# Mask codes of 16 rows instead of 40 in a tree attention kernel

## The chip, the cores and the metric

The kernel runs on one core of a Trainium2 chip. The time is that of the device for one execution, in microseconds (us). Before the change it is 133.4 us, the median of three runs (132.78 to 133.66).

The core's engines work side by side and are kept in step by semaphores: TensorE for matmuls and transposes (PE in the profile, its weight loads PEld), VectorE (DVE), ScalarE (ACT), GpSimd (POOL) and SyncE (SP). Transfers to and from the main memory run on 16 DMA engines; here nearly all of them are issued by POOL.

## The reference: attention along a tree

There are 8 batches of 12 heads, so 96 heads, each with 512 positions of 64 values. The positions are the nodes of a binary tree, numbered as in a heap: the parent of node n is (n - 1) // 2. A query may look at itself and at its ancestors only:

```python
    for i in range(seq):
        mask[i, i] = 1
        parent = i
        while parent > 0:
            parent = (parent - 1) // 2
            mask[i, parent] = 1

    scores = np.einsum('bhqd,bhkd->bhqk', Q, K) * scale
    scores = scores + (1 - mask) * (-1e9)
    weights = np.exp(scores - np.max(scores, axis=-1, keepdims=True))
    weights = weights / (np.sum(weights, axis=-1, keepdims=True) + 1e-10)
    return np.einsum('bhqk,bhkd->bhqd', weights, V)
```

So of 512 x 512 scores per head at most ten in each row count.

## The kernel before

**Heads and pairs.** The work goes in 48 pairs of heads (`i` in the code). The two heads of a pair, `a` = 0 and 1, lie beside each other in the partitions: head 0 has its 64 dimensions in partitions 0 to 63, head 1 in 64 to 127. Four pairs share loads of eight heads.

**Which scores are computed.** The 512 nodes are split by the remainder modulo 4 into four slots of 128. For every query two tiles of 128 keys are enough. The first, in `scores1`, is the top of the tree, nodes 0 to 127. The second, in `scores2`, is a tile of four blocks of 32 nodes in which all the deeper ancestors of the queries of a slot lie; which four blocks it takes depends on the slot (`UNITS`, `TILE2`). Of the four blocks, two neighbours hold nodes from 128 to 255 and the other two hold nodes from 256 up, so that a query finds at most one of its nodes in either two.

**The mask as a matmul.** The mask is not added by VectorE. Before the keys are multiplied with the queries, a product of two small code matrices is put into the same accumulator: `k1code` with `q1code` (L484) under the first scores (L489), `k2code` with `q2code` (L509) under the second (L515). A code product is zero where the key is an ancestor of the query or the query itself, and a large negative number elsewhere (multiples of 2048), so that the exponential gives zero. In the first scores a key's code is its path from the root, as signs, in seven rows, and the negative length of that path in an eighth. In the second scores the code of before has ten rows for each of the four slots, nine signs of the path and one length: 40 rows. The codes are one constant, `tree_codes`, of `CODE_ROWS` rows and 1280 columns. It is loaded once (L183), copied by ScalarE to partitions 64 and up for the second head (L209), and POOL makes a reordered copy `qcoarse` of the query codes for heads 32 and up (L237).

**The stages of a pair.**
- Transpose, T (`transpose`): K and Q come in with nodes in the partitions; TensorE turns them against a permuted unit matrix (L345, L367, L388) into the buffer `kqp`, and VectorE copies that into `kq` (L426, L434, L440).
- Scores, S: per pair two code products of 512 columns (L484), two key products of 512 (L489), two code products of 480 (L509) and eight key products of 160 or 64 columns (L515), always in the order head 0, head 1. ScalarE takes the exponential of the first scores (L500) and of the second (L531).
- Values, V: 12 products of 65 columns with all 128 queries of a slot and 8 with halves of 64 queries (L542); the 65th column sums the weights. VectorE takes the reciprocal (L575) and multiplies (L580).

**What sets the order.** The order on each engine is written by hand. The main loop goes over the turns `i`; a string of letters gives the steps of a turn: by `STV` the scores of pair i are followed by the transposes of a pair ahead and the values of pair i - 1 (`SVT` in the first turns, `FIRST` in the very first). The score buffers `s1` and `s2`, the transposes' `kqp` and the values' `ob` exist once each, so a stage waits for the engine that empties the buffer. Further work of VectorE is to spread V into the order of the tiles (L298, shared with ScalarE and POOL) and, once in four pairs, to lay the two heads' keys beside each other (`Kbeside`, L322). POOL has a list of its own: loads (L249, L259), its share of the V copies, the same laying beside of Q (`Qbeside`, L322), and the stores of the output (L589), which stay 64 heads behind the loads. Its transfers go through eight lanes, and a new one waits for a lane.

Of the kernel before, what the change touches and what calls it, by code (L numbers as in the profile page):

```python
# [9 lines left out]

CODE = 2048.0
CODE_ROWS = 40
NOUT = 10
BEHIND = 64
LANES = 8
# [11 lines left out]
TOP = 6  # L27
TILE2 = (0, 12, 10, 2)

SELF = (2, 3, 2, 3)  # L30
ORDER = (2, 0, 3, 1)
PLACE = (1, 3, 0, 2)
# [28 lines left out]
def _nodes(u0):  # L61
    return np.concatenate(
        [4 * (ROWS[kind] + np.arange(32)) + t for kind, t in UNITS[u0:u0 + 4]]
    )


def _path(n):

    return [1.0 if c == "1" else -1.0 for c in bin(n + 1)[3:]]


def _mask_codes():

    k1 = np.zeros((64, 128), np.float32)
    q1 = np.zeros((64, 4, 128), np.float32)
    k2 = np.zeros((64, 128), np.float32)  # L80
    q2 = np.zeros((64, 4, 128), np.float32)

    def key(codes, row, bits, col, node):
        path = _path(node)
        assert len(path) <= bits
        codes[row:row + len(path), col] = np.array(path) * CODE
        codes[row + bits, col] = -len(path) * CODE

    def query(codes, row, bits, col, node):
        path = _path(node)[:bits]  # L90
        codes[(slice(row, row + len(path)),) + col] = path
        codes[(row + bits,) + col] = 1.0

    for c, node in enumerate(_nodes(TOP)):
        key(k1, 0, 7, c, node)
    for t in range(4):
        for c, node in enumerate(_nodes(TILE2[t])):
            key(k2, 10 * t, 9, c, node)
        for p in range(128):
            node = 4 * p + t  # L100
            query(q1, 0, 7, (PLACE[t], p), node)
            if p >= 32:
                query(q2, 10 * (SELF[t] if p < 64 else t), 9, (PLACE[t], p), node)
    return np.concatenate([k1, q1.reshape(64, -1), k2, q2.reshape(64, -1)], axis=1)


# [8 lines left out]
def kernel(  # L115
# [31 lines left out]
    perm_dram = nc.inline_tensor(_eye_twice().astype(ml_dtypes.bfloat16), name="tree_eye")  # L147
    code_dram = nc.inline_tensor(
        _mask_codes()[0:CODE_ROWS].astype(ml_dtypes.bfloat16), name="tree_codes"
    )  # L150

# [23 lines left out]
    def first_load(eng, name, src):  # L175
        eng.dma_start(
            out=first[name][:, :, :, :].rearrange("p h t d -> p h (t d)"), in_=src[:, 0:2, :]
        )
# [3 lines left out]
    first_load(nc.scalar, "Q", Qr)  # L182
    nc.sync.dma_start(out=codes[0:CODE_ROWS, :], in_=code_dram.ap())  # L183
    eye = ptile[:, 0:256]
# [23 lines left out]

    nc.scalar.copy(out=codes[64:64 + CODE_ROWS, :], in_=codes[0:CODE_ROWS, :])  # L209

# [23 lines left out]
    def code_order(rows):  # L234
        for n, code in enumerate((q1code, q2code)):
            src = code[rows:rows + CODE_ROWS, :].rearrange("r (t p x) -> r x t p", t=4, x=4)
            nc.gpsimd.tensor_copy(out=qcoarse[rows:rows + CODE_ROWS, n, :, :, :], in_=src)  # L237

# [230 lines left out]
    def query_codes(i, a, n, lo, hi):  # L469

        g = i // GP
        rows = slice(64 * a, 64 * a + CODE_ROWS)
        if g in COARSE:
# [347 lines left out]
```

## Time and profile before

| | |
|---|---|
| median of three runs | 133.4 us (132.78 to 133.66) |
| the profiled execution | 134.61 us |
| its span, first to last instruction | 132.7 us |
| TensorE busy | 116.3 us in 2131 matmuls, mean clock 0.984 |
| VectorE, ScalarE, POOL busy | 106.0, 98.4 and 93.2 us |
| read from and written to main memory | 37.92 and 12.58 MB |
| first and last scores begin | 7.13 and 122.49 us |
| last instruction of VectorE ends | 126.8 us |

The profile is one execution, taken by the hardware. Times in it are microseconds from the first instruction. In a group, the form such as `40*128 40x512` gives first the rows and columns of the weights, then the partitions and columns of the stream. "x64 | 12.5, 386 | 0.0" are 64 instructions, 12.5 us busy in sum, 386 ns for one, and no idle time before them. The ends of matmuls are modelled, so consecutive matmuls overlap in it; the distance from one start to the next says how long one really holds the engine. The view of the chain follows the work that ended last backwards; there a step takes the time from the end of the step before.

### The profile page before, as it was taken

Reading aid. Unit: us, or ns where it says so; the run is one execution under the profiler, and the core shown is the slowest. Engines: PE = TensorE matmul, PEld = TensorE weight load, DVE = VectorE, ACT = ScalarE, POOL = GpSimd, SP = SyncE. Lnnn points to the kernel's source line nnn. Section 1 sums busy time; section 2 is a strip of 40 time slices with the busy share of each in tenths; the row PEclk is TensorE's granted clock in tenths of the full one; section 3 lists DMA queues with packets and bytes.
Section 4 is the critical chain, followed back from the end, with each engine's and each line's share of the span. In section 5 each row is a group of like instructions: output and inputs, shape, how many; then the busy total and the mean of one; then the engine's idle time right before and its main releaser. Section 6 shows DMA issues by size and latency. Waiting matters only on the chain.

```text
span 132.7 us, 4957 instructions
## 1 busy us (share of the span) xinstructions
PE 116.3 (88%) x2131; PEld 82.0 (62%) x2131; DVE 106.0 (80%) x216; ACT 98.4 (74%) x153; POOL 93.2 (70%) x140
## 2 busy tenths in 40 slices
PE   6989998898978989999996999999999989999700
PEld 2343765575746667776674786877776757757500
DVE  2427778789896988999999999999999999983610
ACT  4359499799897778799697587887877776889600
POOL 6977735446499999999697974249999998626200
PEclk9999999999999999999999999999999999999985
DMA  3999999999999999999999999999999999999991
GB/s 107 219 183 194 199 194 198 195 198 197 204 203 211 202 203 199 209 206 205 211 200 213 201 342 233 202 332 245 204 316 263 269 396 388 391 381 404 388 357 41
DMA packets 29431, 32.20 MB, mean 243 GB/s; under 512 B 1210, under 2 KB 22330, under 8 KB 29410
## 3 DMA queue, kind: packets, MB, share of 16 engines
q0 software_dynamic: 28112, 30.68, 114.6%
q1 hardware_dynamic: 738, 0.76, 1.6%
q10 hardware_dynamic: 560, 0.46, 1.1%
q8 instruction: 16, 0.26, 0.7%
q14 instruction: 5, 0.04, 0.1%
HBM read 37.92 MB, written 12.58 MB: 380 GB/s over the span
## 4 chain that ended last, share of the span: by engine, by line
DMA 43%; POOL 20%; PE 14%; DVE 9%; ACT 6%; issue 5%; ACTq 0%; POOLq 0%
DMA qst<-in_Q_dram 21%; DMA kst<-in_K_dram 11%; DMA vst<-in_V_dram 11%; POOL vt L298 7%; PE ob L542 5%; DVE of L580 3%; ACT e L531 2%; ACT e L500 2%; DVE vt L298 2%; POOL out_dram L589 2%; POOL qcoarse L237 2%; POOL vst L249 2%; POOL Qbeside L322 2%; PE s L484 2%; PE s L489 1%
## 5 line engine op out<-in xcount | busy, mean ns | idle before, releaser
L500 ACT ACTIVATE e<-s 128x1024 bf16<-128x1024 f32 x48 | 49.2, 1025 | 22.6 <-PE s L489 22.2
L531 ACT ACTIVATE e<-s 128x384 bf16<-128x384 f32 (+1 forms) x80 | 40.8, 556 | 0.0
L542 PE MATMUL ob<-vt,e 128*128 128x65 bf16 (+1 forms) x940 | 37.0, 197 | 2.1 <-DVE of L580 1.3
L542 PEld LDWEIGHTS <-e 128*128 128x128 bf16 (+1 forms) x960 | 30.9, 102 | 8.2 <-DVE of L580 3.4
L580 DVE TENSOR_TENSOR of<-ob,rec 128x512 f32<-128x512 f32 x44 | 30.4, 692 | 1.5
L298 POOL COPY vt<-vst 32x256 uint32<-32x256 uint32 (+1 forms) x52 | 26.2, 503 | 5.5 <-DMA vst<-in_V_dram 3.1
L298 DVE COPY vt<-vst 32x512 uint32<-32x512 uint32 (+4 forms) x52 | 24.7, 475 | 2.8 <-DMA vst<-in_V_dram 1.4
L515 PEld LDWEIGHTS <-kq 64*128 64x128 bf16 x384 | 16.1, 106 | 7.0
L589 POOL DMA_DIRECT2D out_dram<-of x22 | 16.7, 764 | 4.6 <-DVE of L580 2.9
L489 PE MATMUL s<-kq 64*128 64x512 bf16 x96 | 18.6, 379 | 1.0 <-DVE kq L440 0.5
L515 PE MATMUL s<-kq 64*128 64x64 bf16 (+1 forms) x384 | 17.9, 210 | 0.0
L322 POOL COPY Qbeside<-qst 128x1024 uint32<-128x1024 uint32 x9 | 9.7, 1074 | 7.1 <-DMA qst<-in_Q_dram 6.8
L440 DVE COPY kq<-kqp 128x1024 bf16<-128x1024 bf16 x16 | 11.0, 685 | 4.6 <-PE kqp L345 4.4
L575 DVE RECIPROCAL rec<-ob 128x8 f32<-128x8 f32 x47 | 9.4, 199 | 6.0 <-PE ob L542 5.4
L249 POOL DMA_DIRECT2D vst<-in_V_dram x14 | 12.4, 884 | 1.7 <-DVE rec L575 0.7
L484 PE MATMUL s<-qcoarse,codes 40*128 40x512 bf16 x64 | 12.5, 386 | 0.0
L509 PE MATMUL s<-qcoarse,codes 40*128 40x480 bf16 x64 | 12.0, 364 | 0.4 <-ACT e L531 0.2
L509 PEld LDWEIGHTS <-codes 40*128 40x128 bf16 x96 | 7.1, 95 | 8.1 <-issue 2.8
L426 DVE COPY kq<-kqp 128x1024 bf16<-128x1024 bf16 x16 | 11.1, 692 | 1.2 <-PE kqp L388 0.6
L298 ACT COPY vt<-vst 64x512 uint32<-64x512 uint32 (+4 forms) x22 | 11.2, 508 | 0.8 <-DMA vst<-in_V_dram 0.4
L434 DVE COPY kq<-kqp 128x1024 bf16<-128x1024 bf16 x16 | 10.9, 682 | 0.4 <-PE kqp L367 0.3
L367 PE MATMUL kqp<-mixed,Kbeside 128*128 128x128 bf16 x128 | 9.9, 220 | 1.1 <-DVE Kbeside L322 0.8
(43 smaller groups left out, 124.6 us busy)
## 6 DMA issues: line engine op xcount, KB each, us to landing
out_dram<-of POOLq DMA_DIRECT2D x22, 512.0 KB, 9.7
vst<-in_V_dram POOLq DMA_DIRECT2D x11, 512.0 KB, 12.4
qst<-in_Q_dram POOLq DMA_DIRECT2D x10, 512.0 KB, 13.7
kst<-in_K_dram POOLq DMA_DIRECT2D x9, 512.0 KB, 13.5
kst<-in_K_dram POOLq DMA_DIRECT2D x4, 256.0 KB, 9.2
qst<-in_Q_dram POOLq DMA_DIRECT2D x2, 256.0 KB, 9.0
out_dram<-ol POOLq DMA_DIRECT2D x2, 256.0 KB, 7.2
kst<-in_K_dram POOLq DMA_DIRECT2D x3, 128.0 KB, 7.8
```

Source lines behind the costliest of these rows:

```text
L249: return nc.gpsimd.dma_start(out=kept[b][:, h0 % size:h0 % size + n, :, :].rearrange("p h t d -> p h (t d)"), in_=src[:, h0:h0 + n, :],)
L298: return copy(out=dst, in_=src)
L322: copy(out=dst, in_=src)
L484: nc.tensor.matmul(out=columns(g, sp[:, a, :], 0, 512), lhsT=k1code[64 * a:64 * a + CODE_ROWS, :], rhs=query_codes(i, a, 0, 0, 512), start ...
L489: nc.tensor.matmul(out=columns(g, sp[:, a, :], 0, 512), lhsT=keys(i, a, TOP), rhs=queries(i, a, 0, 512), start=False, stop=True,)
L500: nc.scalar.activation(out=dst, in_=src, func=AF.Exp, scale=scale)
L509: nc.tensor.matmul(out=columns(g, flat[:, a, :], 32, 512), lhsT=k2code[64 * a:64 * a + CODE_ROWS, :], rhs=query_codes(i, a, 1, 32, 512), s ...
L515: nc.tensor.matmul(out=columns(g, flat[:, a, :], lo, hi), lhsT=keys(i, a, TILE2[t]), rhs=queries(i, a, lo, hi), start=False, stop=t == 1,)
L531: nc.scalar.activation(out=dst, in_=src, func=AF.Exp, scale=scale)
L542: nc.tensor.matmul(out=ob[lo:hi, a, 65 * t:65 * t + 65], lhsT=e[:, a, PLACE[t], lo:hi], rhs=vt[:, head(i, a) % VB, tile_v, 0:D + 1], **flags,)
L580: nc.vector.tensor_tensor(out=dst, in0=o4[:, a:a + n, :, 0:D], in1=rec[:, a:a + n, :, :].to_broadcast([P, n, 4, D]), op=ALU.mult,)
L589: return eng.dma_start(out=Or[:, h:h + n, :], in_=ofs[h // KB][:, h % KB:h % KB + n, :, :].rearrange("p h t d -> p h (t d)"),)
```

## The change

The number of code rows goes from 40 to 16. The first scores keep their code of eight rows. In the second scores a key's code is no longer its path: it is the place of its column within a block of 32, as five signs, and a weight for its block. Blocks 0 and 1 share rows 0 to 4 for the signs, blocks 2 and 3 share rows 5 to 9, and rows 10 to 13 hold one weight for each block; 14 rows are in use. The query's code has, for a block in which it has an ancestor, the signs of that ancestor's place and a weight of -5, and for any other block a weight of -7. The sum is zero for the ancestor and at most -2 x 2048 for any other key. All of it is computed on the host when the kernel is built; the code matrices have other numbers, and the instructions that read them work on 16 partitions in place of 40. Lines below the function move down by 12.

```diff
-CODE_ROWS = 40
+CODE_ROWS = 16
@@ _mask_codes
-    def key(codes, row, bits, col, node):
+    for c, node in enumerate(_nodes(TOP)):
         path = _path(node)
-        assert len(path) <= bits
-        codes[row:row + len(path), col] = np.array(path) * CODE
-        codes[row + bits, col] = -len(path) * CODE
-
-    def query(codes, row, bits, col, node):
-        path = _path(node)[:bits]
-        codes[(slice(row, row + len(path)),) + col] = path
-        codes[(row + bits,) + col] = 1.0
-
-    for c, node in enumerate(_nodes(TOP)):
-        key(k1, 0, 7, c, node)
+        assert len(path) <= 7
+        k1[:len(path), c] = np.array(path) * CODE
+        k1[7, c] = -len(path) * CODE
+
+    def bits(place):
+        return np.array([1.0 if place >> n & 1 else -1.0 for n in range(5)])
+
+    for c in range(128):
+        block, place = divmod(c, 32)
+        row = 5 * (block // 2)
+        k2[row:row + 5, c] = bits(place) * CODE
+        k2[10 + block, c] = CODE
     for t in range(4):
-        for c, node in enumerate(_nodes(TILE2[t])):
-            key(k2, 10 * t, 9, c, node)
         for p in range(128):
             node = 4 * p + t
-            query(q1, 0, 7, (PLACE[t], p), node)
-            if p >= 32:
-                query(q2, 10 * (SELF[t] if p < 64 else t), 9, (PLACE[t], p), node)
+            path = _path(node)[:7]
+            q1[:len(path), PLACE[t], p] = path
+            q1[7, PLACE[t], p] = 1.0
+            if p < 32:
+                continue
+            up = [node]
+            while up[-1] > 0:
+                up.append((up[-1] - 1) // 2)
+            q2[10:14, PLACE[t], p] = -7.0
+            tile_nodes = _nodes(TILE2[SELF[t] if p < 64 else t])
+            found = [divmod(c, 32) for c in range(128) if tile_nodes[c] in up]
+            assert len({block // 2 for block, _ in found}) == len(found)
+            for block, place in found:
+                row = 5 * (block // 2)
+                q2[row:row + 5, PLACE[t], p] = bits(place)
+                q2[10 + block, PLACE[t], p] = -5.0
```

## The prediction

> **What bounds the kernel now.** I read the page first (busy shares, the row of DMA engines, the chain), then the busy time by stretches, and then the chain of waits at the end and the timeline of VectorE. The page shows no idle engine:
>
> ```profile
> span 132.7 us, 4957 instructions
> ...
> PE 116.3 (88%) x2131; PEld 82.0 (62%) x2131; DVE 106.0 (80%) x216; ACT 98.4 (74%) x153; POOL 93.2 (70%) x140
> ...
> DMA  3999999999999999999999999999999999999991
> ...
> DMA 43%; POOL 20%; PE 14%; DVE 9%; ACT 6%; issue 5%; ACTq 0%; POOLq 0%
> ```
>
> The DMA engines carry packets in every slice, and the chain passes through transfers most often. But such a share says little of who waits, so I go by stretches. Columns: stretch, its length, then busy time with instruction counts of PE, PEld, DVE, ACT, POOL, the granted clock, the DMA share and GB/s:
>
> ```profile
> 21.00:36.00 15.00, 13.81 (x312) 9.95 (x312) 12.57 (x27) 13.30 (x20) 6.86 (x10) 1.00 1.45 198
> 36.00:49.00 13.00, 10.96 (x200) 7.93 (x194) 11.15 (x22) 10.89 (x15) 12.47 (x21) 1.00 1.26 204
> 49.00:73.50 24.50, 22.86 (x422) 16.73 (x420) 22.92 (x42) 19.48 (x32) 22.08 (x34) 1.00 1.23 206
> 73.50:116.70 43.20, 41.87 (x806) 31.72 (x801) 41.30 (x81) 33.69 (x57) 33.39 (x50) 1.00 1.14 292
> ```
>
> From 49 to 116.7 us VectorE is busy 64.2 of 67.7 us and TensorE 64.7 (its ends are modelled, so that is a little too much). VectorE's beat can be read from the copy that it makes once in four pairs:
>
> ```profile
> 80.09 0.83 DVE L322 COPY Kbeside<-kst 128x1024 uint32<-128x1024 uint32 x1
> ...
> 107.71 1.00 DVE L322 COPY Kbeside<-kst 128x1024 uint32<-128x1024 uint32 x1
> ```
>
> With two more between them (four in all), three periods take 27.62 us, so 9.2 us for four pairs. TensorE's own beat, with nothing to wait for, stands in the chain (start, duration, step; a step's time runs from the end of the step before):
>
> ```profile
> 109.60 0.79 PE ob L542 x20
> ...
> 112.50 0.32 PE s L484 x2
> 112.83 0.22 PE s L489 x2
> 113.04 0.21 PE s L509 x2
> 113.25 0.21 PE s L515 x8
> 113.46 0.55 PE kqp L388 x8
> 114.01 0.61 PE ob L542 x20
> ```
>
> One pair is the sum of the last six rows, 2.12 us, and four pairs are 8.48. So in the long middle VectorE is the bound by a small margin (9.2 against 8.48, that is 0.18 us a pair); before it the loads and POOL's copies are, where POOL is busy 12.47 of 13 us from 36 to 49; and from 109.60 us on the chain lies on TensorE, later on ScalarE too.
>
> **The change, part by part.** No instruction is added, removed or moved: the order on every engine is the same. What changes is the height of the code operands, 40 rows to 16, in the code transfer, its copies and the code products.
>
> ```profile
> L484 PE MATMUL s<-qcoarse,codes 40*128 40x512 bf16 x64 | 12.5, 386 | 0.0
> ...
> L237 POOL COPY qcoarse<-codes 40x512 bf16<-40x512 bf16 x4 | 2.8, 736 | 0.0
> ```
>
> *The code transfer and its copies.* The first code product against ScalarE's copy:
>
> ```profile
> 4.64 1.26 ACT L209 COPY codes<-codes 40x1280 bf16<-40x1280 bf16 x1 [1.42 <-DMA codes<-tree_codes]
> ...
> 6.78 0.41 PE L345 MATMUL kqp<-ptile,kst 128*64 128x128 bf16 x8 [0.25 <-DVE kq L440]
> ...
> 7.13 0.39 PE L484 MATMUL s<-codes 40*128 40x512 bf16 x2
> ```
>
> The transfer of 40 rows becomes one of 16 and may land earlier than at 4.64; ScalarE's copy waits 1.42 us for it and ends at 5.90. That gains nothing: the first code product starts at 7.13, 1.2 us later, behind transposes that waited for VectorE.
>
> The copies have the same elements per partition, only fewer partitions. For ScalarE two rows show that the partitions don't count:
>
> ```profile
> L298 ACT COPY vt<-vst 64x512 uint32<-64x512 uint32 x7 | 4.4, 627 | 0.1
> ...
> L298 ACT COPY vt<-vst 32x512 uint32<-32x512 uint32 x5 | 3.1, 627 | 0.1
> ```
>
> For POOL's four copies no such pair stands in the trace. Bounds: nothing, or in proportion to the rows, 24/40 of 2.8 = 1.7 us gained in a stretch where POOL issues loads into DMA engines that are full anyway. I take 0, by the ScalarE rows, the nearest; from the ends I keep −1.7.
>
> *The code products.* The streams stay 512 and 480 columns, so the matmuls themselves stay as long, and two of them run side by side already (the row at 7.13 has two in 0.39 us, where one is 0.386). What does change is the part of the array that they occupy. The built program places every product in a tile by its rows and columns. Until now codes (40 rows) and keys (64 rows) both took the 64 by 128 tile, one at row 0, one at row 64. With 16 rows the codes take a 32 by 128 tile, so the four groups of a pair's scores now go 32, 64, 32, 64 rows where they went 64, 64, 64, 64.
>
> What does such a change of tile cost? The trace has three a pair, and the chain above prices them. L484 and L489 stream the same 512 columns, yet the first takes 0.32 and the second 0.22: L484 follows value products in a 128 by 64 tile, L489 follows its own kind. So 0.10 us. L388 streams 8 x 128 = 1024 columns; at L489's 512 in 0.22 that is 0.44, and it takes 0.55: 0.11 for 64 by 128 to 128 by 128. L542 has 12 products of 65 columns and 8 that go in pairs, 1040 columns or 0.45 us, and takes 0.61: 0.16 for one change inside it, its small starts included. L509, which follows its own kind of tile, takes 0.21 for 480 columns, which is 0.206 by the same rate: no price. So 0.10 to 0.16 for each change, and I take 0.10, since two of three lie there and the new ones sit between long streams as at L484. No row has a change between 64 and 32 rows; its bounds are 0 and 0.16.
>
> The Trainium skill ("TensorEngine Tiling (Array Packing)", Tiling Modes) says that a change of tiling mode, not of the tile alone, drains TensorE, and lists 64 and 32 rows as different modes; the three prices above agree with the drain, and no run here shows the 64 to 32 case yet. It speaks against this change, and by it the sum stays the one below.
>
> New changes per pair: before L489, before L509, before L515. L484 had one and keeps one. That is 3 x 0.10 = 0.30 us a pair, and 48 x 0.30 = 14.4 us of TensorE time in all. Nothing is removed from it.
>
> **How much of it reaches the end.** By stretches, with these starts of a pair's scores (pairs 0 as quoted, 15, 44):
>
> ```profile
> 49.03 0.39 PE L484 MATMUL s<-codes 40*128 40x512 bf16 x2
> ...
> 116.67 0.39 PE L484 MATMUL s<-qcoarse,codes 40*128 40x512 bf16 x2
> ```
>
> *Middle, pair 15 to 44*: 29 pairs in 67.64 us. TensorE's beat becomes 2.12 + 0.30 = 2.42, four pairs 9.68, above VectorE's 9.2: the bound changes hands. 29 x 2.42 = 70.2 us, so +2.5 if TensorE never waits. It will still wait: in the turn with the extra copy VectorE gets some 0.8 us of work more, and the next value products need the buffer that it empties. From that I take 0.2 us per four pairs, 7 times, 1.4 us: now the wait there is about 9.2 − 8.48 = 0.7, and TensorE's beat grows by 0.3 on each of two turns around it. That makes +3.9. Bounds: +2.5, and 29 x 0.30 = +8.7 where every wait of today stays.
>
> *Beginning, pair 0 to 15*: 41.9 us, 15 x 0.30 = 4.5 added. TensorE's waits are for loads, and the chain there runs through them:
>
> ```profile
> 11.48 9.48 DMA qst<-in_Q_dram
> ...
> 27.58 0.24 PE s L489 x2
> ...
> 32.73 0.38 PE s L509 x2
> 33.10 0.20 PE s L515 x8
> ...
> 34.79 0.24 PE s L489 x2
> ...
> 49.89 13.96 DMA vst<-in_V_dram
> ```
>
> Between the two transfers the chain passes four of the new changes (L489, L509, L515, L489), 0.4 us; the rest lies in waits for transfers that don't start earlier or later by it. Because loads are issued behind buffers that TensorE empties, a little more leaks through: I take +0.9, bounds 0 and 4.5.
>
> *End, from pair 44*: no transposes are left, and the chain alternates between ScalarE and TensorE:
>
> ```profile
> 117.09 0.42 PE s L489 x2
> ...
> 118.51 0.88 ACT e L531 x2
> ...
> 119.43 0.38 PE s L509 x2
> 119.81 0.20 PE s L515 x8
> ...
> 121.06 0.24 PE s L489 x2
> ...
> 123.22 0.38 PE s L509 x2
> 123.60 0.21 PE s L515 x8
> ```
>
> L489, L509 and L515 stand in it twice each: 6 x 0.10 = +0.6. The last values, norms and stores only shift.
>
> Sum: 0.9 + 3.9 + 0.6 = +5.4 us. The profiled execution took 134.6 us (span 132.7 and 1.9 around it), which lies 1.2 above the median of 133.4; against itself it would be 140.0, against the median 138.8.
>
> **The rivals.**
>
> *A, the other side: no drain between 64 and 32 rows.* If a 32-row tile is only half of the 64-row one to the array, a pair stays at 2.12 us. More generally, VectorE's 9.2 us for four pairs hide the change as long as 8.48 + 12c stays below it, so up to c = 0.06 us; below that only six changes in the end count, at most 0.4 us, and POOL's shorter copies may take 1.7 us off. For it: no row shows such a change. Against it: three different changes of tile, in rows and in columns, all cost 0.10 or more. Time 133.4, range 131.7 to 133.8; not slower.
>
> *B, the drain costs what I think, but the waits swallow it.* The chain touches TensorE little before 109.60 us (14% of the whole span). If VectorE and the transfers go on setting the beat up to there, only what the chain passes counts: four new changes early, three in each of the three pairs from 109.60 on, six at the end, 19 x 0.10 = +1.9, so 135.3. For it: the chain's shares and the DMA row. Against it: from 73.5 us TensorE is idle for only 1.3 us of 43.2, and 9.68 is more than 9.2; there is hardly a wait to hide in.
>
> *C, nothing is hidden.* All waits are fixed distances behind TensorE's own work (a single score buffer, a single value buffer, loads behind buffers), and the 14.4 us add in full: 147.8. For it: the buffers are single. Against it: VectorE's 0.7 us in four pairs is a bound of its own and is overtaken, not added to; C is the forecast with that step failed.
>
> **How the numbers follow.** The forecast, 138.8, reaches from 136.5 (0 + 2.5 + 0.6) to 143.6 (0.9 + 8.7 + 0.6) by its own bounds and has 0.68. A has 0.10, B 0.13, and C with all that lies above 143.6 has 0.09; a price of 0.16 in place of 0.10 is in these, since it would lead there. The range of 134.8 to 145.0 leaves out A (0.10), an edge of B, and most of C, about 0.2 in all. About 1% is what a measurement of this kernel can tell from no change. Slower by over 1% (above 134.7): forecast, C and nearly all of B, 0.88. Within 1%: most of A and an edge of B, 0.10. Faster by over 1%: A with POOL's 1.7 us reaching the end, 0.02.
>
> **What the new profile would show.** L489, L509 and L515 as steps of the chain at about 0.32, 0.31 and 0.31 us where TensorE runs without a wait, L484 still at 0.32, and a pair at 2.42; the duration of L484 in its group unchanged (386 ns), since the drain lies between instructions. VectorE with small waits for TensorE in the middle, where it has none now, and the four-pair beat of its extra copy at 9.7 to 9.9. POOL's L237 still at 0.7 us each. I would be wrong if L489 stays at 0.22 behind L484 (A), if the beat stays at 9.2 (B), or if it reaches 10.4 (C).

## The result and the profile after

The changed kernel takes 139.29 us (median of six runs, 138.32 to 141.41) against 133.31 (132.78 to 134.67): by the medians it is slower by 6.0 us, where 5.4 was forecast (138.8 us in all). The ratio is 1.040, with a 95% interval of 1.036 to 1.045, which is 5.4 us (4.8 to 6.0). Here and below a ratio compares only the faster executions of both kernels (within 1.5% of the fastest of their kind), so it is not the quotient of the medians. The profiled execution took 139.53 us.

The page of the changed kernel, its heads and the rows of slices (tenths busy; the last is GB/s):

```profile
span 137.7 us, 4957 instructions
...
PE 129.5 (94%) x2131; PEld 81.0 (59%) x2131; DVE 106.7 (77%) x216; ACT 98.4 (71%) x153; POOL 92.5 (67%) x140
...
PEclk9999999999998699999999999999999999999997
DMA  3999999999999999999999999999999999980474
GB/s 110 218 184 195 200 194 197 195 199 198 208 203 213 200 207 208 207 206 208 200 211 204 339 231 206 339 229 206 339 227 332 400 401 399 366 321 23 164 293 152
...
PE 87%; DVE 10%; issue 1%
```

The same 4957 instructions; VectorE, ScalarE and POOL as busy as before, TensorE 129.5 us in place of 116.3, and the chain that ended last lies on TensorE for 87% of the span, where it was on transfers for 43%. In the last four slices the DMA engines are no longer full; before they were until the last but one. (In the 13th and 14th slice TensorE was granted less clock, 8 and 6 tenths, so the beginning reads too long in this execution.)

The chain in the middle, columns as before (start, duration, step). L496, L501, L521 and L527 are the L484, L489, L509 and L515 of before:

```profile
97.58 0.32 PE s L496 x2
97.90 0.34 PE s L501 x2
98.24 0.31 PE s L521 x2
98.55 0.32 PE s L527 x8
98.87 0.55 PE kqp L379 x8
99.42 0.61 PE ob L554 x20
```

The first keeps its 0.32 us, the transposes and values their 0.55 and 0.61. The three steps that follow a group in the other tile are longer by 0.12, 0.10 to 0.11 and 0.11 (they were 0.22, 0.20 to 0.21 and 0.21). A pair is 2.45 us.

VectorE's extra copy, once in four pairs, from the timeline (with two others between these):

```profile
85.31 0.70 DVE L334 COPY Kbeside<-kst 128x1024 uint32<-128x1024 uint32 x1
...
114.98 0.69 DVE L334 COPY Kbeside<-kst 128x1024 uint32<-128x1024 uint32 x1
```

Three periods take 29.67 us, 9.89 for four pairs, against 4 x 2.45 = 9.80 of TensorE's own. VectorE now waits:

```profile
84.58 0.69 DVE L438 COPY kq<-kqp 128x1024 bf16<-128x1024 bf16 x1 [0.45 <-PE kqp L400]
```

And the busy time by stretches (columns as in the prediction), with the stretch behind VectorE's last instruction at the end:

```profile
52.90:73.50 20.60, 20.60 (x345) 13.22 (x342) 18.81 (x36) 16.05 (x27) 18.66 (x29) 1.00 1.22 208
73.50:121.60 48.10, 48.10 (x820) 31.54 (x819) 41.86 (x83) 35.01 (x59) 33.12 (x48) 1.00 1.12 305
121.60:135.10 13.50, 12.26 (x220) 7.61 (x216) 8.59 (x20) 9.71 (x18) 2.94 (x4) 1.00 0.48 187
135.10:137.70 2.60, 0.00 (x0) 0.00 (x0) 0.00 (x0) 0.00 (x0) 0.00 (x0) 0.63 0.41 144
```

The last row has an answer in the profile before that the prediction did not read: there nothing but transfers ran for 5.90 us.

```profile
126.80:132.70 5.90, 0.00 (x0) 0.00 (x0) 0.00 (x0) 0.00 (x0) 0.00 (x0) 0.64 0.48 178
```

The issues show why. The last stores through POOL, before and then after (KB each, median us from issue to landing):

```profile
out_dram<-ol POOLq DMA_DIRECT2D x2, 256.0 KB, 7.2
```

```profile
out_dram<-ol POOLq DMA_DIRECT2D x2, 256.0 KB, 2.9
```

So by this profile pair 15 begins 3.95 us later (52.98 against 49.03; part of it is the clock), the stretch to pair 44 takes 4.03 more (71.67 against 67.64), VectorE's end comes 0.3 later still (10.4 after pair 44's start, 10.1 before), and 3.3 us come back behind it. That is 5.0 in the span. The profiled execution of the kernel before took 134.61 us, 1.3 over its median, so the two profiles lie nearer together than the medians.

### The profile page after: what moved, and what is told of

It reads as the page before. It is cut to its first block, busy times and chain, and to the rows that moved or that the text cites. A ratio compares the mean times of both kernels' runs of the same rounds, so it can differ in the third digit from the quotient of the medians.

```text
span 137.7 us, 4957 instructions
## 1 busy us (share of the span) xinstructions
PE 129.5 (94%) x2131; PEld 81.0 (59%) x2131; DVE 106.7 (77%) x216; ACT 98.4 (71%) x153; POOL 92.5 (67%) x140
## 4 chain that ended last, share of the span: by engine, by line
PE 87%; DVE 10%; issue 1%
PE ob L554 20%; PE s L501 11%; PE s L527 10%; PE s L496 10%; PE s L521 10%; PE kqp L379 6%; PE kqp L400 6%; PE kqp L357 6%; DVE kq L452 3%; PE s L740 3%; DVE vt L310 2%; DVE of L592 2%; PE ob L740 2%; PE s L554 1%; DVE rec L587 1%
## 5 line engine op out<-in xcount | busy, mean ns | idle before, releaser
L554 PEld LDWEIGHTS <-e 128*128 128x128 bf16 (+1 forms) x960 | 31.6, 103 | 5.8 <-issue 1.1
L310 DVE COPY vt<-vst 32x512 uint32<-32x512 uint32 (+4 forms) x52 | 25.9, 498 | 1.5
L501 PE MATMUL s<-kq 64*128 64x512 bf16 x96 | 19.3, 398 | 0.7 <-DVE kq L452 0.7
L527 PE MATMUL s<-kq 64*128 64x64 bf16 (+1 forms) x384 | 18.5, 215 | 0.0
L527 PEld LDWEIGHTS <-kq 64*128 64x128 bf16 x384 | 11.4, 108 | 10.2 <-issue 10.2
L496 PE MATMUL s<-qcoarse,codes 16*128 16x512 bf16 x64 | 12.4, 385 | 0.0
L501 PEld LDWEIGHTS <-kq 64*128 64x128 bf16 x96 | 5.1, 103 | 12.0 <-issue 10.4
L521 PE MATMUL s<-qcoarse,codes 16*128 16x480 bf16 x64 | 12.0, 372 | 0.0
L521 PEld LDWEIGHTS <-codes 16*128 16x128 bf16 x96 | 4.6, 91 | 10.9 <-issue 10.9
```

Of the source, the lines that this page charges most:

```text
L310: return copy(out=dst, in_=src)
L496: nc.tensor.matmul(out=columns(g, sp[:, a, :], 0, 512), lhsT=k1code[64 * a:64 * a + CODE_ROWS, :], rhs=query_codes(i, a, 0, 0, 512), start ...
L501: nc.tensor.matmul(out=columns(g, sp[:, a, :], 0, 512), lhsT=keys(i, a, TOP), rhs=queries(i, a, 0, 512), start=False, stop=True,)
L521: nc.tensor.matmul(out=columns(g, flat[:, a, :], 32, 512), lhsT=k2code[64 * a:64 * a + CODE_ROWS, :], rhs=query_codes(i, a, 1, 32, 512), s ...
L527: nc.tensor.matmul(out=columns(g, flat[:, a, :], lo, hi), lhsT=keys(i, a, TILE2[t]), rhs=queries(i, a, lo, hi), start=False, stop=t == 1,)
L554: nc.tensor.matmul(out=ob[lo:hi, a, 65 * t:65 * t + 65], lhsT=e[:, a, PLACE[t], lo:hi], rhs=vt[:, head(i, a) % VB, tile_v, 0:D + 1], **flags,)
```

## The experiments

The theory: each change between a 64-row and a 32-row tile stops TensorE for about 0.11 us, VectorE's own beat hides the first of them, and a delay of the computation costs the total only what goes beyond some 3.3 us, since the kernel before ends on a backlog of stores (stores that were issued and have not landed). The rivals: the new numbers and smaller copies, or the number of rows itself; that changes add in full; and that the last stores simply take 5.9 us.

**Rows at the edge of the tile.** Two kernels with the new codes, filled up with rows of zeros:

```diff
-CODE_ROWS = 16
+CODE_ROWS = 33     # 32 in the second kernel
```

> The new codes, padded with rows of zeros to 33, so that the code products are placed in the 64 by 128 tile again. If the change of tile costs the time: as before, 133.3 us (132.6 to 134.0), L501 0.22 us behind L496. If the new numbers, the smaller transfer or the copies cost it: near 139.3.

> The same codes padded to 32 rows, the most that still fits the 32 by 128 tile. If the tile decides: 139.3 us (138.3 to 140.3). If the number of rows itself did, in proportion: a third of the way from 40 rows to 16, about 135.3, and the run with 33 rows about the same.

With 33 rows the ratio to the kernel before is 1.005 (1.001 to 1.010), with 32 rows 1.033 (1.025 to 1.042): of 133.3 us that is 134.0, the upper edge of what was expected, and 137.7, a little under it. With 33 rows the first key products start 0.23 us behind the codes:

```profile
52.16 0.39 PE L496 MATMUL s<-codes 33*128 33x512 bf16 x2
52.39 0.38 PE L501 MATMUL s<-kq 64*128 64x512 bf16 x2
```

With 32 rows the chain has the steps of the changed kernel:

```profile
110.89 0.32 PE s L496 x2
111.21 0.34 PE s L501 x2
111.55 0.31 PE s L521 x2
111.85 0.32 PE s L527 x8
```

One row of zeros more decides. The numbers, the transfer and the copies are not the cause, nor is the number of rows in proportion. (POOL's four reordering copies take 694 ns each in the median with 16 partitions, 735 with 40: of the bound of −1.7 us, 0.2 is there.)

**One, two or three changes a pair.** With 40 rows loaded, one of the two code products is given only the first 16 (the edit abridged; `k2code` is cut in the same way by `code_rows(i, 1)`):

```diff
+    def code_rows(i, n):
+        return (16, 40)[n]     # (40, 16) in the second kernel
...
-        rows = slice(64 * a, 64 * a + CODE_ROWS)
+        rows = slice(64 * a, 64 * a + code_rows(i, n))
...
-lhsT=k1code[64 * a:64 * a + CODE_ROWS, :]
+lhsT=k1code[64 * a:64 * a + code_rows(i, 0), :]
```

> Only the first code products (L496) take 16 rows, the second take 40: one new change of tile a pair. If VectorE's 9.2 us for four pairs hide TensorE's 8.48 + 0.40: 133.3 to 134.3 us. If every change adds in full: 133.3 + 48 x 0.10 = 138.1.

> Only the second code products (L521) take 16 rows: two new changes a pair. TensorE's four pairs 8.48 + 0.80 = 9.28, just over VectorE's 9.2: 134.0 to 136.0 us. If every change adds in full: 142.9; if two of three changes cost two thirds of the loss: 137.3.

With the first codes alone (one change) the ratio is 1.002 (0.996 to 1.007), with the second alone (two) 1.010 (0.995 to 1.025). Both lie inside the expected times (133.5 and 134.7 us, of 133.3), far from 138.1 and 142.9; the upper end of the second, 136.6, is only just under the 137.3 of two thirds of the loss. The chain shows the price move with the change. In these kernels the lines stand four further down: L500, L505, L525 and L531. First codes alone; here the first key products L505 pay, the second codes L525 don't:

```profile
110.75 0.04 issue
110.80 0.79 PE ob L558 x20
111.58 0.32 PE s L500 x2
111.90 0.34 PE s L505 x2
112.24 0.20 PE s L525 x2
```

Second codes alone; L505 is cheap, L525 and L531 pay:

```profile
109.76 0.32 PE s L500 x2
110.08 0.22 PE s L505 x2
110.30 0.31 PE s L525 x2
110.61 0.32 PE s L531 x6
```

From the starts of pairs 15 and 44 the middle takes 67.8 us with none (33 rows), 68.4 with one, 69.7 with two, 72.1 with three (32 rows). The first change costs 0.6, a fifth of its 29 x 0.11 = 3.2 us, the second 1.3, the third 2.4: they come out of VectorE's cover one after the other. These are single profiles: in those of the old tile with the whole clock in this stretch the middle takes 67.2 to 67.8, in those with three changes 71.7 to 73.1.

**The same 32-row products, fewer changes.** The four code products of a pair are put together, so that two of three new changes go (the edit abridged):

```diff
+        s2s[i] = codes2(i)     # second code products, ahead of the first key products
         for a in range(2):
             nc.tensor.matmul(
                 out=columns(g, sp[:, a, :], 0, 512), lhsT=keys(i, a, TOP),
```

> 16 rows, but the four code products of a pair stand together, then the two and eight key products: one new change of tile a pair in place of three, with the same 32-row products. If the price is that of the change: TensorE's beat 2.12 + 0.10 = 2.22 us a pair, 8.9 for four pairs, under VectorE's 9.2, so 133.3 to 134.5 us in all. If 32-row products are slow in themselves: 139.3. A loss by another way, the second code products waiting for their buffer in front of the first key products, would show as waits for ScalarE, at most 0.2 us a pair in the late stretch.

This was a miss: 146.2 us in the fastest of four executions, and 152.0 to 152.5 in the others, so there is no ratio with an interval. The chain, in a stretch with the whole clock, shows a wait that I had put at 0.2 us a pair:

```profile
93.21 0.88 ACT e L553 x2
94.09 0.04 issue
94.13 0.38 PE s L524 x2
94.51 0.36 PE s L502 x2
...
94.95 0.16 ACT e L513
95.11 0.76 issue
95.87 0.88 ACT e L553 x2
```

The second code products (L524) must wait until ScalarE has emptied their buffer (L553), and the first key products (L502) now stand behind them; ScalarE needs those for its first exponential (L513). From L553 to L553 the ring takes 2.66 us, and nothing overlaps in it (the 0.76 us of issue is the rest of the first exponential, before the second can start). To see whether the ring or the 32-row products were slow, the same order was run in the old tile:

```diff
-CODE_ROWS = 16
+CODE_ROWS = 33     # with the codes first
```

> The order with the four code products first, with 33 rows, so in the old tile and with no new change of tile. In the 16-row run of that order a pair took 2.66 us: ScalarE's exponential of the second scores, the second code products, the first key products and ScalarE's two exponentials follow each other in a ring. If the ring is the cause, it stays, shorter by the one change of tile in it: about 2.55 us a pair and 142 to 148 us in all. If the 32-row products were the cause: 133.3 to 134.5.

The ratio is 1.047 (1.037 to 1.057): three executions took 140.0 to 141.8 us. The order loses without any new change of tile. That is a little under the expected 142, and about 6 us under the 16-row run of the same order, of which one change of tile in a ring of 48 turns would be 48 x 0.11 = 5.3. The fourth execution, the profiled one, took 534.8 us with code products of 1342 ns in the median and can't show the ring; that it is the same ring in the old tile is argued.

**Where the delay arises.** The 16 rows for some pairs only, in both codes (`16 if i < 15 else 40`, and so on):

> Both codes with 16 rows in pairs 0 to 14 only. By the prediction's step for the beginning, pair 15 starts 0.9 us later than at 49.0; by the profile of the changed kernel 3.7 later. By the first 134.2 us in all; by the second, with a store backlog at the end that takes up to 3.3 us of delay, 133.5 to 134.5, and the time behind VectorE's last instruction 2.6 to 4 us instead of 5.9.

> Both codes with 16 rows in pairs 15 to 43 only. From pair 15 to 44 about 71.6 us instead of 67.6 either way. If the stores behind the last values take as long as before: 133.3 + 3.9 = 137.2 us. If the delay is first taken from a backlog of stores (up to 3.3 us): 134.0 to 135.3, with 2.6 us behind VectorE's last instruction.

> Both codes with 16 rows in pairs 44 to 47 only. The prediction's step for the end, six changes in the chain, makes +0.6 us: 133.9 against 133.3, or ratio 1.005. If the end of the kernel before waits for a backlog of stores, VectorE ends 0.3 to 0.6 us later and the total doesn't move: ratio 1.000.

Ratios: pairs 0 to 14 0.996 (0.989 to 1.003); pairs 15 to 43 1.024 (1.013 to 1.035), 3.2 us; pairs 44 to 47 1.001 (0.996 to 1.006). They add up to 2.8 us, about half of the loss of all together: each alone meets the same slack at the end. The first lies under both of its expected times and rests on three executions; its profile, with less clock in two slices of the beginning, has pair 15 at 53.65, VectorE's end at 130.8 and 2.6 us behind it, so 4.0 us of delay and 0.7 more in the span. The last can't tell 1.005 from 1.000. In the middle alone the delay was larger than either theory had it: the stretch takes 73.1 us (pair 15 at 50.30, pair 44 at 123.41), since TensorE kept some waits there, as at pair 20, which takes 3.00 us; VectorE ends at 133.33 and 2.64 us later all is over. 6.5 us late, less 3.3 of slack, is 3.2. Of the 6.5, 1.3 arise ahead of pair 15, where nothing was changed, and are spread between runs. So 134.0 to 135.3 was too low because of the middle and 137.2 right in size by a wrong path; that the waits stay because TensorE comes to that stretch earlier than in the changed kernel is argued, not shown.

**The stores at the end.** Four of POOL's 22 stores are left out, once in the old tile and once in the new one, so 16 heads of the output are not written (the old tile has `CODE_ROWS = 33` besides):

```diff
-        ops += [(store, nc.gpsimd, q) for q in range(stored, NQ - 2)]
+        ops += [(store, nc.gpsimd, q) for q in range(stored + 4, NQ - 2)]
```

> 33 rows (the old tile), with four of the 22 POOL stores left out (16 heads of the output are not written). If the last stores of the kernel before sit behind a backlog of stores: the time from VectorE's last instruction to the end falls from 5.9 us to about 2.6, and the whole from 133.3 to 129.5 to 131.0 us. If that time is what a last store takes anyway: 133.3.

> The changed kernel with the same four stores left out (16 heads of the output are not written). If the changed kernel has no backlog of stores left at its end: as the changed kernel, ratio 1.035 to 1.045 to the kernel before, where the same omission with the old tile gave 0.986. If the transfers bound both kernels alike: 0.014 less than the changed kernel, about 1.026.

In the old tile the ratio is 0.986 (0.977 to 0.995), in the new one 1.040 (1.030 to 1.050), as with all stores. In the old tile the last stores land in 2.9 us instead of 7.2 and the span ends 2.6 us behind VectorE:

```profile
out_dram<-of POOLq DMA_DIRECT2D x18, 512.0 KB, 9.9
...
out_dram<-ol POOLq DMA_DIRECT2D x2, 256.0 KB, 2.9
```

The gain, some 1.9 us, is less than the 2.3 to 3.8 expected, in part because VectorE's end came at 127.6 instead of 126.8. The backlog is there before, and gone after. Its size is less sure: 3.3 us is read from one execution of the kernel before, 1.3 over its median, while the omission gained 1.9 us over the runs (0.6 to 3.1).

The run with 33 rows gives the same answer in another way. TensorE was granted less clock in two slices of its beginning (its page):

```profile
PEclk9999999999995599999999999999999999999998
```

Pair 15 starts at 52.16, in the row above. That is 3.1 us behind the kernel before, and VectorE ends 3.1 us later, at 129.92; yet the span is 132.6 us, as before. 3.1 us of delay went into the backlog.

The other profiles with all stores agree. With 32 rows, with the second codes alone, and with the early or the middle pairs changed, VectorE ends 4.0 to 6.8 us later than before, the span is 0.7 to 3.5 us longer, and 2.6 to 2.7 us follow VectorE's end each time. Two fit less well: with the first codes alone VectorE ends 1.8 us later and the span is 0.6 longer; with the late pairs alone changed, under a mean clock of 0.85, 4.4 and 1.8.

## Why the prediction was right, and where it was not

- **The change of tile holds TensorE: right.** No row of before had a change between 64 and 32 rows; the price by its neighbours, 0.10 us, is 0.10 to 0.12 by the chain. Rival A fell with it. The rule of the Trainium skill ("TensorEngine Tiling (Array Packing)", Tiling Modes), that changing the mode drains TensorE, agrees with the runs with 33 and 32 rows; they show the time, not that a drain is what takes it.
- **VectorE's beat as cover: right.** One change at 0.11 us costs four pairs 0.44, under the 0.7 that VectorE left over, and four fifths of it were hidden; three were not. The limit of 0.06 us that rival A gives is the same 0.7, shared by the twelve new changes of four pairs.
- **The middle: right, in parts that cancel.** Forecast +3.9, measured +4.0. The beat was 2.45 instead of 2.42, 0.9 us more over 29 pairs, and the wait left over 0.09 us in four pairs instead of 0.2, 0.8 us less.
- **The beginning: perhaps too small.** The step "a little more leaks through: I take +0.9" can't be judged to the half microsecond. With the first pairs in the new tile and the whole clock, pair 15 begins at 51.0 (32 rows) and 51.7 (16 rows, fewer stores). In the old tile it begins at 49.0 before, but at 50.2 (33 rows, fewer stores) and 50.3 (the middle pairs alone changed) in two other runs. The means differ by 1.5 us, single runs by 0.7 to 2.7.
- **The end: the step that failed.** "The last values, norms and stores only shift." The values and norms did, by 0.3 us where I had 0.6. The stores did not: behind VectorE's last instruction the kernel before has 5.9 us and the changed one 2.6. I took the time there for a fixed cost, though the issue table of before has the last stores at 7.2 us.

So the total was right in part by luck. Three changes a pair delay VectorE's end by more than the 5.4 us of the sum: by 6.8 us with 32 rows and 8.3 with 16, the latter with less clock in its beginning. That was made up for by a backlog that I had not seen, 3.3 us in these profiles. Rival B, too, was right in its reason, that transfers bound the kernel before, but at another place: not that waits in the middle swallow the change, but that the end has a backlog to give. Rival C's 14.4 us fell: even VectorE's end is delayed by no more than 8.3 us, and the loss is 6.0.

## What to carry to other kernels

An operand that gets smaller can cost time on TensorE when its height falls from 33 rows to 32 and it alternates with operands of 64 rows: count the changes of tile per turn, not the rows. Padding with zeros to 33 rows kept the tile here and cost 0.1 to 1.0% against the 40 rows of before. And look at what runs behind the last instruction of the computation before a delay is added to the total: a backlog of stores there takes a delay up. By the same reasoning an edit that makes the computation earlier would gain nothing until the backlog is gone; no run here made it earlier.

## What the runs showed that was not expected

- A change between the 64 by 128 and 32 by 128 tiles holds TensorE for 0.10 to 0.12 us in either direction, as much as the changes to 128 rows or 64 columns (0.10 to 0.16). The durations of the matmuls hardly show it: the first key products, whose step grows by 0.12 us, take 402 ns in the median (L501) against 377 before (L489). The distance of the starts does. The sign that the prediction named for this, an unchanged duration of L484, tests nothing, since L484 had its change of tile already.
- With single score buffers the order of four short products matters as much as the tile: setting the second code products ahead of the first key products closed a ring through ScalarE in the 16-row run, and cost 4.7% (3.7 to 5.7) even where it changed no tile.
